# Rotary embedding on one core: four slots of 32 KB for x in place of five, batch 7 loaded and batch 4 stored in halves, the last 1 MB stored as two transfers

## The chip, the cores and the metric

The kernel runs on one core of one Trainium2 chip. The metric is the device time of one execution in microseconds. Before the change the median of three executions is 164.32 us (163.64, 164.32 and 164.39). One further execution was profiled. It took 164.17 us, and its profile spans 162.4 us from the first to the last instruction, so 1.8 us of the time lie outside the span.

## The reference: what is computed

The input `x` has the shape (8, 2048, 8, 64) in float32: 8 batches, 2048 positions, 8 heads, 64 elements a head. `cos` and `sin` have the shape (2048, 32).

```python
x1 = x[..., :32]
x2 = x[..., 32:]
out1 = x1 * cos - x2 * sin
out2 = x1 * sin + x2 * cos
return np.concatenate([out1, out2], axis=-1)
```

`cos` and `sin` are the same for all batches and heads of a position. x is 33.55 MB and so is the output. Each element is read once and written once.

## The kernel before, in words

**Tiling.** A batch is one tile `xt` of 128 partitions by 8192 floats (`ROW`, 32 KB in each partition, 4 MB in all). Partition q holds the 16 positions 16q to 16q+15, each of 512 floats (`HD`), so a partition's row of a batch is one contiguous run of 32 KB in DRAM, both for the load and for the store. The tiles come from `xpool`, which has `NBUF` slots. The rotation is done in place, and the store reads the same tile, so a slot is free for a new batch when the store of the old batch has landed.

**Loads.** `load(b)` issues the loads of batch b on the SP queue. Batch 0 comes as three transfers (1, 1 and 2 MB, rows of 8, 8 and 16 KB) with the table of cosines between them; the other batches come as one transfer of 4 MB with rows of 32 KB. The first `NBUF` batches are loaded ahead of everything (line 77). The load of batch b + `NBUF` is issued after the stores of batch b in program order (line 192); on SP it waits for those stores' landing. SP's instructions stand in a fixed order, so what is behind a waiting load waits too. Two of the early loads also wait for another transfer because eight completion semaphores are handed round: in the kernel before, the load of batch 4 waits for the first 1 MB of batch 0's store.

**Compute.** `rotate` treats a piece of 2048 floats a partition (`UNIT`, four positions); batch 0 begins and batch 7 ends with two pieces of half that. The order on each engine is the program's order (`keep`). There are three kinds of piece. Kind A: POOL makes `t2` in two multiplications (line 122), DVE makes `t1` (line 129) and adds the two into x (line 136). Kind B (the first piece of batches 2, 4 and 5): POOL and DVE make `t2` and `t1`, and TensorE and ScalarE add and copy back. Kind C (the first piece of batches 1 and 3): DVE makes both products, and POOL has none. `t2` has three buffers, so POOL can run at most some pieces ahead of DVE.

**Stores.** `shares(b)` says in which transfers a batch is stored: batch 0 in four of 1 MB, batches 1 to 6 in one of 4 MB each, batch 7 in three of 2, 1 and 1 MB (rows of 16, 8 and 8 KB). Each is issued when its pieces are done. Batches 0 to 6 go out on the ACT queue, batch 7 on the SP queue, behind all the loads. SP's and ACT's queues (q1 and q10 in the profile) feed the same 16 DMA engines.

Of the kernel before, what the change touches and what calls it, by code (L numbers as in the profile page):

```python
# [10 lines left out]
def kernel(  # L11
# [15 lines left out]
    HD = H * D  # L27
    R = S // P
    ROW = R * HD
    UNIT = 4 * HD  # L30
    NBUF = 5
    C = 512
    last = B - 1

# [9 lines left out]
    t1s_pool = ctx.enter_context(tc.tile_pool(name="t1s", bufs=2))  # L44
    xpool = ctx.enter_context(tc.tile_pool(name="xpool", bufs=NBUF))
    t2_pool = ctx.enter_context(tc.tile_pool(name="t2p", bufs=3))
# [11 lines left out]
    def spans(sizes):  # L58
        lo = 0
        for n in sizes:  # L60
            yield lo, n
            lo += n

    def load(b):
        xt = xpool.tile([P, ROW], f32, tag="xt", name=f"xt{b}")
        for lo, n in spans([UNIT, UNIT, 2 * UNIT] if b == 0 else [ROW]):
            keep(nc.sync.dma_start(out=xt[:, lo : lo + n], in_=xv[b, :, lo : lo + n]))
            if b == 0 and lo == 0:
                keep(nc.sync.dma_start(out=cos_sb, in_=cos_src))
        xts[b] = xt  # L70

    def store(b, lo, n):
        queue = nc.sync if b == last else nc.scalar
        keep(queue.dma_start(out=ov[b, :, lo : lo + n], in_=xts[b][:, lo : lo + n]))

    keep(nc.scalar.dma_start(out=sin_sb, in_=sin_src))
    for b in range(NBUF):
        load(b)
# [98 lines left out]
    def shares(b):  # L177
        if b == 0:
            return [UNIT] * 4
        if b == last:  # L180
            return [2 * UNIT, UNIT, UNIT]
        return [ROW]

    for b in range(B):
        done = 0
        outs = list(spans(shares(b)))
        for lo, n in spans(pieces(b)):
            rotate(b, lo, n)
            done = lo + n
            while outs and sum(outs[0]) <= done:  # L190
                store(b, *outs.pop(0))
        if b + NBUF <= last:
            load(b + NBUF)

# [29 lines left out]
```

## Time and profile before

| what | value |
|---|---|
| median of three executions | 164.32 us |
| profiled execution, its own time | 164.17 us |
| span of the profile | 162.4 us |
| DVE busy | 140.1 us, 86% |
| POOL busy | 138.8 us, 85% |
| PE busy, ACT busy | 49.1 us, 12.8 us |
| DMA moved | 67.65 MB, mean 417 GB/s |
| share of 16 engines' span, q1 and q10 | 55.1% and 42.5% |
| last DVE addition ends | 151.89 us |
| last store issued, landed | 151.91 us, 161.49 us |

The trace gives each transfer an issue and a landing (the time at which all 16 DMA engines have reported). In order, in us, with the transfer's size:

```
load 0    0.73, 1.63, 2.10 -> 6.10, 9.25, 14.12   (1, 1, 2 MB)
load 1    2.68 ->  25.86    store 0  12.71 -> 28.88, 18.16 -> 40.97,
load 2    6.11 ->  37.98             22.89 -> 53.17, 27.61 -> 62.90 (1 MB each)
load 3    9.26 ->  50.15    store 1  46.12 ->  78.80
load 4   28.89 ->  62.28    store 2  62.35 ->  99.07
load 5   63.03 ->  86.98    store 3  80.81 -> 118.78
load 6   78.88 -> 106.73    store 4  97.05 -> 132.36
load 7   99.15 -> 126.32    store 5 113.51 -> 142.05
                            store 6 132.47 -> 154.78
                            store 7 142.01 -> 156.60 (2 MB), 146.73 -> 159.04,
                                    151.91 -> 161.49 (1 MB each)
```

A busy share counts an engine's own instructions. The share of a DMA queue counts the time of its packets, summed over the 16 engines; one packet is one partition's row of a transfer, and each engine takes eight of a transfer's 128 rows. Where both queues have work, an engine alternates between them.

### The profile page before, as it was taken

To read this page: it belongs to the slowest core of one execution; us is meant where nothing else is said; L and a number is where in the kernel's file an instruction comes from. 1 tells how busy PE (TensorE), PEld (TensorE's weight loads), DVE (VectorE), ACT (ScalarE), POOL (GpSimd) and SP (SyncE) were. 2 spreads that over 40 slices of the span, in tenths; PEclk is the share of its full clock that TensorE was granted. 3 is DMA by queue.
4 is the path that set the end of the run, shared out by engine and by line. 5 is a ranking of instruction groups with operands and counts; after the bars stand their busy time and mean duration, and the time that the engine had idled before them with its cause. 6 is when DMAs were issued, how large, how long until landed. Compare 5 with 4: busy or idle time off the path is not lost.

```text
span 162.4 us, 462 instructions
## 1 busy us (share of the span) xinstructions
PE 49.1 (30%) x80; PEld 18.5 (11%) x80; DVE 140.1 (86%) x66; ACT 12.8 (8%) x14; POOL 138.8 (85%) x70
## 2 busy tenths in 40 slices
PE   0000000597209750977058805971000000000000
PEld 0000000233003210322022302230000000000000
DVE  0397999999999999999999999999999999999300
ACT  3300000002200220022001120022000000000000
POOL 1499997999999999999995999999999999993000
PEclk9999999999965997589857995699555555555555
DMA  5999799899899899989999999899999999999992
GB/s 182 426 426 517 337 470 452 363 476 460 353 478 468 349 474 476 396 388 509 388 388 501 404 438 460 388 460 438 396 476 420 396 484 412 396 460 428 396 428 113
DMA packets 3602, 67.65 MB, mean 417 GB/s; under 512 B 400, under 2 KB 400, under 8 KB 656
## 3 DMA queue, kind: packets, MB, share of 16 engines
q1 hardware_dynamic: 2016, 38.01, 55.1%
q10 hardware_dynamic: 1584, 29.62, 42.5%
q14 instruction: 2, 0.02, 0.0%
HBM read 34.08 MB, written 33.55 MB: 417 GB/s over the span
## 4 chain that ended last, share of the span: by engine, by line
DVE 75%; POOL 9%; issue 6%; DMA 3%; DVEq 0%
DVE t L129 40%; DVE xt L136 33%; POOL t L122 9%; DMA sin_sb<-in_sin_dram 3%; DVE t L148 3%; DVEq L136 0%
## 5 line engine op out<-in xcount | busy, mean ns | idle before, releaser
L122 POOL TENSOR_TENSOR t<-xt,sin_sb 128x1024 f32<-128x1024 f32 (+1 forms) x32 | 70.7, 2210 | 8.2 <-DMA sin_sb<-in_sin_dram 5.0
L129 DVE TENSOR_TENSOR t<-xt,cos_ps 128x2048 f32<-128x2048 f32 (+1 forms) x34 | 73.4, 2166 | 0.8
L122 POOL TENSOR_TENSOR t<-xt,nsin 128x1024 f32<-128x1024 f32 (+1 forms) x32 | 70.7, 2211 | 0.0
L136 DVE TENSOR_TENSOR xt<-t,t 128x2048 f32<-128x2048 f32 (+1 forms) x29 | 62.2, 2145 | 4.2 <-POOL t L122 1.2
L143 PE MATMUL o<-t,eye 128*128 128x512 f32 x24 | 16.9, 794 | 23.2 <-DVE t L129 19.7
L160 PE MATMUL o<-t,eye 128*128 128x512 f32 x16 | 12.0, 842 | 37.6 <-DVE t L129 35.4
L144 PE MATMUL o<-t,eye 128*128 128x512 f32 x24 | 14.9, 709 | 0.0
L145 ACT COPY xt<-o 128x1024 f32<-128x1024 f32 x6 | 6.1, 1012 | 45.7 <-PE o L144 34.9
L143 PEld LDWEIGHTS o<-t,eye 128*128 128x128 f32 x24 | 5.6, 257 | 32.6 <-issue 26.7
L160 PEld LDWEIGHTS o<-t,eye 128*128 128x128 f32 x16 | 3.7, 257 | 43.1 <-issue 39.2
L165 ACT COPY xt<-o 128x1024 f32<-128x1024 f32 x4 | 4.0, 1012 | 47.7 <-PE o L161 47.7
L144 PEld LDWEIGHTS o<-t,eye 128*128 128x128 f32 x24 | 5.6, 235 | 8.0 <-issue 7.5
L93 DVE COPY cos_ps<-cos_sb 128x512 f32<-128x512 f32 x1 | 0.7, 695 | 6.8 <-DMA cos_sb<-in_cos_dram 6.8
L161 PE MATMUL o<-t,neye 128*128 128x512 f32 x8 | 6.2, 870 | 0.2
L148 DVE TENSOR_TENSOR t<-xt,sin_ps 128x2048 f32<-128x2048 f32 x2 | 4.6, 2280 | 0.0
L161 PE MATMUL o<-t,eye 128*128 128x512 f32 x8 | 4.1, 593 | 0.0
L161 PEld LDWEIGHTS o<-t,neye 128*128 128x128 f32 x8 | 2.1, 294 | 5.2 <-issue 3.6
L161 PEld LDWEIGHTS o<-t,eye 128*128 128x128 f32 x8 | 1.5, 190 | 1.9 <-issue 1.9
L90 ACT ACT_TABLE_LOAD x1 | 1.3, 1283 | 1.2 <-PEq L208 1.2
L90 ACT ACTIVATE nsin<-sin_sb 128x512 f32<-128x512 f32 x1 | 0.6, 629 | 3.9 <-DMA sin_sb<-in_sin_dram 3.9
L91 ACT COPY sin_ps<-sin_sb 128x512 f32<-128x512 f32 x1 | 0.6, 579 | 0.0
L80 POOL MEMSET eye<- 128x128 f32 x1 | 0.2, 206 | 0.3 <-POOLq L208 0.3
(6 smaller groups left out, 1.0 us busy)
## 6 DMA issues: line engine op xcount, KB each, us to landing
xt<-in_x_dram SPq DMA_DIRECT2D x7, 4096.0 KB, 27.9
out_dram<-xt ACTq DMA_DIRECT2D x6, 4096.0 KB, 34.0
out_dram<-xt ACTq DMA_DIRECT2D x4, 1024.0 KB, 26.5
xt<-in_x_dram SPq DMA_DIRECT2D x2, 1024.0 KB, 6.5
xt<-in_x_dram SPq DMA_DIRECT2D x1, 2048.0 KB, 12.0
out_dram<-xt SPq DMA_DIRECT2D x1, 2048.0 KB, 14.6
out_dram<-xt SPq DMA_DIRECT2D x2, 1024.0 KB, 10.9
sin_sb<-in_sin_dram ACTq DMA_DIRECT2D x1, 256.0 KB, 5.5
```

The source lines that it names most:

```text
L90: keep(nc.scalar.mul(nsin, sin_sb, -1.0))
L93: keep(nc.vector.tensor_copy(cos_ps, cos_sb))
L122: nc.gpsimd.tensor_mul(out=t2u[:, :, u, :].rearrange("p (r h) d -> p r h d", h=H), in0=xu[:, :, 1 - u, :].rearrange("p (r h) d -> p r h d" ...
L129: nc.vector.tensor_mul(out=t1.rearrange("p (r k d) -> p r k d", r=nr, d=Dh), in0=xk, in1=rep(cos_ps[:, r0 : r0 + nr, :], 2 * H),)
L136: keep(nc.vector.tensor_add(out=xt, in0=t1, in1=t2))
L143: nc.tensor.matmul(oc, eye, t1[:, cs], start=True, stop=False)
L144: nc.tensor.matmul(oc, eye, t2[:, cs], start=False, stop=True)
L145: keep(nc.scalar.copy(xt[:, 2 * j * C : 2 * (j + 1) * C], o))
L148: nc.vector.tensor_mul(out=t2.rearrange("p (r k d) -> p r k d", r=nr, d=Dh), in0=xk, in1=rep(sin_ps[:, r0 : r0 + nr, :], 2 * H),)
L160: nc.tensor.matmul(oc, eye, t1u[:, gs, u, :], start=True, stop=False)
L161: nc.tensor.matmul(oc, eye if u else neye, t2u[:, gs, 1 - u, :], start=False, stop=True)
L165: nc.scalar.copy(xu[:, :, u, :], o.rearrange("p (g d) -> p g d", d=Dh))
```

## The change

`xpool` has four slots in place of five, which leaves 32 KB of each partition unused. The first four batches are loaded ahead; the load of batch b + 4 waits for the landing of batch b's store. Batch 7 is loaded as two transfers of 2 MB with rows of 16 KB. Batch 4 is stored as two transfers of 2 MB with rows of 16 KB, the first of them after the batch's second piece. The last 1 MB of batch 7 is stored as two transfers of 512 KB with rows of 4 KB, one after each of the two half pieces. The order of the compute instructions on DVE, POOL, TensorE and ScalarE is the same.

```diff
-    NBUF = 5
+    NBUF = 4
@@ load
-        for lo, n in spans([UNIT, UNIT, 2 * UNIT] if b == 0 else [ROW]):
+        for lo, n in spans({0: [UNIT, UNIT, 2 * UNIT], last: [2 * UNIT, 2 * UNIT]}.get(b, [ROW])):
             keep(nc.sync.dma_start(out=xt[:, lo : lo + n], in_=xv[b, :, lo : lo + n]))
@@ shares
         if b == 0:
             return [UNIT] * 4
         if b == last:
-            return [2 * UNIT, UNIT, UNIT]
-        return [ROW]
+            return [2 * UNIT, UNIT, 2 * HD, 2 * HD]
+        return [2 * UNIT, 2 * UNIT] if b in (4,) else [ROW]
```

## The prediction, made before the changed kernel was run

> **What bounds the kernel now.** I read the page's rows on DMA first, because 67.65 MB in 162.4 us is much for one core.
>
> ```profile
> DMA  5999799899899899989999999899999999999992
> ...
> q1 hardware_dynamic: 2016, 38.01, 55.1%
> q10 hardware_dynamic: 1584, 29.62, 42.5%
> ...
> DVE 75%; POOL 9%; issue 6%; DMA 3%; DVEq 0%
> ```
>
> The two queues' packets took 55.1 + 42.5 = 97.6% of 16 engines' span, that is 0.976 x 162.4 = 158.5 us on each engine. The last line, the chain that ended last, says something else: DVE 75%. But that chain is followed back from the last instruction, which is DVE's addition that ends at 151.89 us. The 10.5 us after it are not on the chain; they belong to stores. The table of stretches decides between the two readings (the columns are the stretch, its length, busy time and instructions of PE, PEld, DVE, ACT and POOL, PE's clock, the DMA share, GB/s):
>
> ```profile
> 10.00:25.00 15.00, 0.00 (x0) 0.00 (x0) 13.82 (x8) 0.00 (x0) 14.94 (x8) 1.00 0.99 418
> 63.00:80.00 17.00, 10.15 (x16) 3.64 (x16) 16.62 (x8) 2.02 (x2) 17.00 (x8) 0.80 1.00 430
> 100.00:125.00 25.00, 9.03 (x16) 3.31 (x14) 23.99 (x11) 2.02 (x2) 25.00 (x12) 0.70 0.98 424
> 125.00:142.00 17.00, 0.00 (x0) 0.00 (x0) 16.36 (x8) 0.00 (x0) 17.00 (x8) 0.50 1.00 432
> 142.00:152.00 10.00, 0.00 (x0) 0.00 (x0) 9.49 (x6) 0.00 (x0) 5.65 (x5) 0.50 1.01 434
> 152.00:160.00 8.00, 0.00 (x0) 0.00 (x0) 0.00 (x0) 0.00 (x0) 0.00 (x0) 0.50 0.89 378
> ```
>
> The DMA engines have no idle time from 10 us to 152 us, with loads and stores, with loads alone nearly, and with stores alone. They carry on after the last DVE instruction, and their rate (418 to 434 GB/s) hardly depends on the mix. So the time is the DMA work plus the 1 us before its start and the last landing. Compute matters only where it lets the DMA engines run dry. From the packets, 14 of the engines finish between 159.2 and 159.8 us and the slowest at 161.1 us.
>
> Who waits for slots is in SyncE's waits and in the single issues:
>
> ```profile
> SPq L67 <- DMA out_dram<-xt: 88.1, 4, 33.6
> ...
> 28.89 0.33 SPq L67 DMA_DIRECT2D xt<-in_x_dram  x1
> ...
> 63.03 0.33 SPq L67 DMA_DIRECT2D xt<-in_x_dram  x1
> ...
> 99.15 0.33 SPq L67 DMA_DIRECT2D xt<-in_x_dram  x1
> ...
> 151.91 0.33 SPq L74 DMA_DIRECT2D out_dram<-xt  x1
> ```
>
> The loads of batches 4, 5 and 7 are issued at 28.89, 63.03 and 99.15 us (6 at 78.88), each just after the landing of a store. And two lines show who needs the loads first, and where POOL holds DVE already (POOL's first multiplication for batch 4; DVE's addition for the second piece of batch 5):
>
> ```profile
> 71.79 2.40 POOL L122 TENSOR_TENSOR t<-xt,sin_sb 128x1024 f32<-128x1024 f32 x1
> ...
> 101.70 2.29 DVE L136 TENSOR_TENSOR xt<-t,t 128x2048 f32<-128x2048 f32 x1 [0.33 <-POOL t L122]
> ```
>
> **Part 1: four slots.** Load 4 now waits for all of store 0, and loads 5, 6, 7 for stores 1, 2, 3 in place of 0, 1, 2. They stand in order on SP, so each also waits for those ahead. I work the queue forward by one rule read off the landings: the engines alternate row by row between the queues, and a 4 MB transfer alone takes 4.19 MB / 432 GB/s = 9.7 us (1.21 us a row), beside another of 32 KB rows 19.4 us.
>
> - Load 3 lands at 50.15 us as before. The SP queue is then empty, and the ACT queue has a fifth of store 0's third MB and its fourth MB left, 3 us alone. It ends near 52 and lands near 53.4: load 4 is issued there, 24.5 us later than before.
> - Store 1 (issued at 46.12) runs from 52, alone for three rows, then beside load 4 for five: it ends near 67.8, lands near 69.2. Load 5 is issued there (before: 63.03).
> - Load 5 of before, in the same company, took 86.98 - 63.03 = 23.95 us to land. So load 4 lands near 53.4 + 23.9 = 77.3. Load 6 of before, behind 8 us of another load, took 27.85 us; so load 5 lands near 69.2 + 27.85 = 97.0.
> - Store 2 ends near 67.8 + 19.4 = 87.2, load 6 is issued near 88.6. It has 2:1 company once store 4's 16 KB rows come, and lands near 114.5. Store 3 lands near 108, and load 7's halves land near 124 and 136.
>
> POOL wants load 4 at 71.79 and gets it at 77.3. It runs two multiplications of 2.29 us a piece, so batch 4's second piece is ready at 77.3 + 9.2 = 86.5; DVE's addition there stood at 85.22, so DVE loses 1.3 us. POOL is through with batch 4 at 95.6 and waits for load 5 until 97.1; the second piece of batch 5 is ready at 97.1 + 9.2 = 106.3, where DVE's addition stood at 101.70. DVE is then 4.6 us late in all. Batch 6 is wanted by POOL at 115.4 (there near 114.5) and batch 7 at 133.7 and 142.8 (there at 124 and 136): nothing more. The last addition ends near 151.89 + 4.6 = 156.5 us.
>
> What is this worth? While compute stalls, the DMA engines always have a load and a store, or one whole 4 MB store, in front of them: at 53 store 1, at 69 load 4 and store 2, at 88 load 5 and store 3, at 108 load 6 and store 4, and from 134 on stores 5, 6 and 7, which lie there in stock. So the cost is 0 as long as the last piece comes before the stock is used up. Before, the typical engine had 159.3 - 2.5 (the last 1 MB) = 156.8 us of work without the last transfer, whose issue at 151.91 left 4.9 us less the 1.0 us from issue to first packet (0.73 to 1.73 at the start), so 3.9 us of cover. The delay of 4.6 us takes all of it and 0.7 us more on the typical engine, if nothing else changed. Part 3 gives 1.2 us back. On the slowest engine there are 1.8 us more.
>
> **Part 2: halves of load 7 and store 4.** Two more transfers; each issue takes 0.33 us on a queue that waits anyway (the cover is SyncE's 88.1 us of waits; without it, 0.33 us each). Row prices in the packets: 32 KB 1.213, 16 KB 0.611, 8 KB 0.309 us. Two rows of 16 KB cost 0.009 us more than one of 32 KB, eight rows an engine: 0.07 us for each transfer split, 0.14 us in all, on the path because the DMA engines are. The first half of store 4 leaves some 3 us earlier; as nothing is idle, that moves work and gains nothing.
>
> **Part 3: the last 1 MB in two.** No row of 4 KB is in the trace. Its bounds are half an 8 KB row, 0.1545 us, and two 2 KB rows (the tables'), 0.168 us; a gain is excluded because the bytes stay. Sixteen rows an engine in place of eight of 0.309: +0.0 to +0.22 us. I take 0.158 (the rows of 8 KB are nearest), +0.06 us. Only 512 KB, 1.27 us, now follow the last addition in place of 2.5: the cover grows by 1.2 us.
>
> **Sum.** 0.14 + 0.06 = +0.2 us of DMA work. The last 512 KB is issued near 156.5, its first row is due near 157.5; the typical engine has work until 159.3 + 0.2 - 1.27 = 158.2. The cover is 0.7 us there and 2.5 us on the slowest engine. So the span goes from 162.4 to 162.6, and the profiled execution's 164.17 to 164.4 us, which is the median of before plus 0.05%: no change that can be told. A measurement of this kernel tells about 0.5%, 0.8 us, from nothing.
>
> By the Trainium skill ("SBUF — State Buffer", "The DMA setup-cost knee") every transfer pays a roughly fixed 2 us; with three transfers more that would be 6 us, 170.4 us. The trace has 25 transfers and no idle DMA engine between 10 and 152 us, so here the fixed part lies in latency and not in the engines' time.
>
> **Rivals.**
>
> 1. *The stock runs dry (slower).* Load 5's landing sets POOL, POOL sets DVE, 1:1, and past the cover the end follows 1:1. On the slowest engine it decides from a last addition at 156.5 + 2.5 = 159.0; on typical engines from 157.2, and they become the last ones past 159. For 0.8 us more than the sum it needs about 159.8, that is load 5 landing 3.3 us later than 97.0, or load 6 later than 118. The landings lag by 2 us behind the rows (load 7 of before reports on 16 engines from 124.4 to 126.3), and each slot now hangs on two such lags. A last addition at 160 to 161 would give 165.4 to 166.3. Against it: load times taken from the trace include that lag once.
> 2. *A shorter tail (faster).* If compute set the end, half of the last transfer would gain 1.2 us: 163.0; 161.1 - 159.3 = 1.8 us is also what the slowest engine could lose of its lag, 162.4. For it: compute does end later now. Against: the last store took 9.6 us to land for 2.5 us of work, so there is a queue in front of it.
> 3. *A price for each transfer.* If every transfer held the engines for its latency: the first 1 MB took 5.4 us to land for 2.5 us of moving, 2.9 us more; three times is 8.7 us, 172.9 us. The full shares of DMA in the stretches speak against it.
> 4. *The freed 32 KB does something by itself:* nothing takes it, so 0 us; it falls together with the forecast.
>
> **How the numbers follow.** Forecast, with rival 4: 0.62. Rival 1: 0.24, rival 2: 0.12, rival 3: 0.02. The likeliest case's own range is 163.7 to 165.0 (the three executions of before differ by 0.75 us; part 3's upper end is 0.2 more). The 8-in-10 range reaches down to 163.4, into rival 2, and up to 166.0, into rival 1. Faster by over 0.5% is under 163.5: 0.12; slower is over 165.1: 0.26 (rivals 1 and 3); between them 0.62.
>
> **What would show it.** The DMA share should stay at 0.98 or more in all stretches from 10 to 156 us. Load 4 should be issued near 53.4, 5 near 69, 6 near 89, 7 near 108; POOL should wait about 5.5 us for load 4 and 1.5 us for load 5; DVE's idle time should grow by about 4.6 us and its last addition end near 156.5. The last store should land 4 to 5 us after its issue, in place of 9.6. The prediction is wrong if the share drops below 0.95 in a stretch before 152, or if the last addition ends past 159.

## The result and the profile after

| | before | changed |
|---|---|---|
| median | 164.05 us (20 executions) | 165.05 us (20 executions) |
| profiled execution | 164.17 us, span 162.4 us | 164.47 us, span 162.7 us |
| last DVE addition ends | 151.89 us | 156.48 us |
| last store issued, landed | 151.91, 161.49 us | 156.50, 161.61 us |

The ratio is 1.0061 with a 95% interval of 1.0043 to 1.0079: slower by 0.6%, at the edge of the 0.5% that the prediction took as the least that can be told. Two later comparisons of the same two kernels, on two chips, gave 1.0029 (1.0008 to 1.0051) and 1.0043 (1.0022 to 1.0063). So the change costs some 0.3 to 0.6%, 0.5 to 1.0 us, and the sum of the prediction had 0.2 us. The first profiled execution, at 164.47 us, is one of the faster of its twenty (164.11 to 165.80); its own difference, 0.30 us, agrees with the sum better than the medians do. Of the changed kernel's 20 executions 10 took over 165.0 us, of the 20 before 2.

The DMA rows of the changed kernel's page and, below them, its chain that ended last in order of time (start, length, what):

```profile
q1 hardware_dynamic: 2304, 38.01, 55.1%
q10 hardware_dynamic: 1728, 29.62, 42.5%
...
46.19 23.05 DMA out_dram<-xt
69.38 27.54 DMA xt<-in_x_dram
...
97.05 9.20 POOL t L122 x4
```

The queues' shares are the same to a tenth of a percent, over a span that is 0.3 us longer. The chain now holds what was not on it before: the store of batch 1, then the load of batch 5 into the slot that this store has freed, then POOL's four multiplications for batch 5, and only then DVE.

The stretches of the changed kernel that answer to those shown of before (columns as there), and the waits and issues:

```profile
63.00:80.00 17.00, 9.15 (x16) 3.20 (x16) 16.62 (x8) 2.02 (x2) 11.77 (x6) 0.86 1.00 430
100.00:125.00 25.00, 9.76 (x16) 3.80 (x16) 21.23 (x10) 2.02 (x2) 25.00 (x12) 0.70 1.00 430
125.00:142.00 17.00, 0.00 (x0) 0.00 (x0) 16.35 (x9) 0.00 (x0) 17.00 (x8) 0.50 1.02 438
142.00:152.00 10.00, 0.00 (x0) 0.00 (x0) 9.72 (x5) 0.00 (x0) 10.00 (x7) 0.50 0.96 413
152.00:160.00 8.00, 0.00 (x0) 0.00 (x0) 4.23 (x4) 0.00 (x0) 0.26 (x1) 0.50 0.95 401
```

```profile
SPq L67 <- DMA out_dram<-xt: 93.4, 4, 39.3
...
53.57 0.33 SPq L67 DMA_DIRECT2D xt<-in_x_dram  x1
...
69.38 0.33 SPq L67 DMA_DIRECT2D xt<-in_x_dram  x1
...
77.28 2.32 POOL L122 TENSOR_TENSOR t<-xt,sin_sb 128x1024 f32<-128x1024 f32 x1 [5.24 <-DMA xt<-in_x_dram]
97.05 2.33 POOL L122 TENSOR_TENSOR t<-xt,sin_sb 128x1024 f32<-128x1024 f32 x1 [1.38 <-DMA xt<-in_x_dram]
...
86.51 2.29 DVE L136 TENSOR_TENSOR xt<-t,t 128x2048 f32<-128x2048 f32 x1 [1.31 <-POOL t L122]
106.28 2.29 DVE L136 TENSOR_TENSOR xt<-t,t 128x2048 f32<-128x2048 f32 x1 [3.22 <-POOL t L122]
...
156.50 0.33 SPq L74 DMA_DIRECT2D out_dram<-xt  x1
```

POOL waits 5.24 us for batch 4 and 1.38 us for batch 5, DVE then 1.31 and 3.22 us for POOL, and the last store is issued at 156.50 us in place of 151.91. POOL's busy time from 63 to 80 us falls from 17.00 to 11.77 us, DVE's from 100 to 125 us from 23.99 to 21.23 us, while the DMA share is 1.00 in both stretches. From 142 to 152 us it reads 0.96: a packet counts whole in the stretch in which it begins, and by the packet records no engine is idle there. Compute is late by 4.6 us, and the DMA engines do not notice it in this execution. This profile accounts for 0.3 us. What is left to find is why the medians differ by more.

### The profile page after: what moved, and what is told of

Its sections match the earlier page's. It is cut to its first block, busy times and chain, and to the rows that moved or that the text cites. A ratio compares the mean times of both kernels' runs of the same rounds, so it can differ in the third digit from the quotient of the medians.

```text
span 162.7 us, 472 instructions
## 1 busy us (share of the span) xinstructions
PE 49.0 (30%) x80; PEld 18.3 (11%) x80; DVE 140.1 (86%) x66; ACT 12.8 (8%) x14; POOL 138.9 (85%) x70
## 3 DMA queue, kind: packets, MB, share of 16 engines
q1 hardware_dynamic: 2304, 38.01, 55.1%
q10 hardware_dynamic: 1728, 29.62, 42.5%
## 4 chain that ended last, share of the span: by engine, by line
DVE 48%; DMA 35%; POOL 11%; issue 1%; DVEq 0%; SPq 0%; POOLq 0%; ACTq 0%
DVE xt L136 24%; DVE t L129 23%; DMA xt<-in_x_dram 17%; DMA out_dram<-xt 14%; POOL t L122 11%; DMA sin_sb<-in_sin_dram 3%; DVE t L148 1%; DVEq L136 0%; SPq L67 0%; POOLq L122 0%; ACTq L74 0%
```

## The experiments

The theories, as they were named at the time: **A**, the late last addition uses up the cover at the end; **B**, the splits cost more than their packets show; **C**, four slots lengthen the slowest DMA engine's lag, whenever compute ends; **D**, a finer form of A, in which the last addition stands just at the edge of the cover and lags of landings push it over; **E**, lateness and splits together. All ratios are to the kernel before, beside which each ran.

| run | slots | splits | last addition ends (its profile) | ratio, 95% interval |
|---|---|---|---|---|
| e1 | 4 | no | 158.4 us | 1.0065, 1.0039 to 1.0091 |
| e2, e11 | 5 | yes | 152.1, 152.5 us | 1.0015, 0.9998 to 1.0033; 1.0021, 0.9997 to 1.0045 |
| e3, e10 | 4 | yes | 153.7, 154.4 us | 1.0033, 1.0007 to 1.0060; 1.0083, 1.0057 to 1.0110 |
| e4 | 5 | no | 156.5 us | 0.9985, 0.9967 to 1.0003 |
| e6 | 5 | yes | 156.8 us | 1.0031, 1.0000 to 1.0062 |
| changed, e7, e9 | 4 | yes | 156.5, 157.8, 157.8 us | 1.0061; 1.0029; 1.0043 |
| e12 | 5 | yes | 158.9 us | 1.0047, 1.0030 to 1.0065 |
| e5 | 4 | yes | 159.6 us | 1.0129, 1.0092 to 1.0166 |

Runs e1 to e4 shared one chip, e5 to e8 a second, e9 to e12 a third. e8 is the changed kernel profiled once more: one execution, 164.59 us, last addition at 157.5 us.

### Four slots alone, and the splits alone

```diff
 e1, from before:    -    NBUF = 5          +    NBUF = 4
 e2, from changed:   -    NBUF = 4          +    NBUF = 5
```

> Four slots alone: load 7, store 4 and the last 1 MB stay whole. Theory A (the cover at the end is used up: the last addition comes some 4.6 us later, and the DMA engines have little or nothing left to do when the last transfer is issued): load 7 whole lands near 136 where POOL wants it near 134, so the last addition comes near 157.5 to 158.5, and 1 MB instead of 512 KB follows it; the ratio to the kernel before is 1.010 to 1.020, worse than the changed kernel's 1.006. Theory B (the three more transfers and the smaller rows cost more than their packets show): 0.998 to 1.002. Theory C (four slots make the slowest DMA engine's lag longer, through the waits for landings, whenever compute ends): about 1.005.

> The three splits with five slots. Theory A: the last addition stays near 151.9 us, the work of the splits is 0.2 to 0.3 us, ratio 1.000 to 1.003. Theory B: the splits carry the loss, 1.004 to 1.008. Theory C: 1.000 to 1.003 as well; e3 tells A from C.

Four slots alone gave 1.0065, the splits alone 1.0015. So the splits cost about what the sum said (0.15% is 0.25 us, the interval runs from 0 to 0.5 us, and the sum had 0.2 us), and B falls as the main cause. In this pair the slots carry the rest. In e1 the load of batch 7, whole, landed at 136.7 us and the last addition came at 158.39, as A expected. The last microseconds (one stretch each, columns as before) show what follows:

```profile
157.00:158.00 1.00, 0.00 (x0) 0.00 (x0) 0.90 (x2) 0.00 (x0) 0.00 (x0) 0.50 0.83 352
158.00:159.00 1.00, 0.00 (x0) 0.00 (x0) 0.40 (x1) 0.00 (x0) 0.00 (x0) 0.50 0.14 57
159.00:160.00 1.00, 0.00 (x0) 0.00 (x0) 0.00 (x0) 0.00 (x0) 0.00 (x0) 0.50 0.90 377
160.00:161.00 1.00, 0.00 (x0) 0.00 (x0) 0.00 (x0) 0.00 (x0) 0.00 (x0) 0.50 1.01 410
```

The DMA share drops to 0.14 for a microsecond: nothing is in front of the engines until the last 1 MB, issued at 158.42, arrives. That is the dry spell of rival 1, in the kernel without the splits. A's size was too large all the same (1.010 to 1.020 expected). The same stretch of the changed kernel's first profile:

```profile
158.00:159.00 1.00, 0.00 (x0) 0.00 (x0) 0.00 (x0) 0.00 (x0) 0.00 (x0) 0.50 1.01 414
```

So in this execution the halves of load 7 and of the last 1 MB do keep the engines from running dry.

### Compute early with four slots, compute late with five

```diff
 e3, from changed, in rotate:
         kind = kinds.get((b, lo), "A")
+        if b == 6 and lo in (UNIT, 2 * UNIT):
+            n = n // 2
 e4, from before, after the multiplication of line 129:
+        if b == 5 and lo in (UNIT, 2 * UNIT):
+            keep(nc.vector.tensor_mul(...))      # the same once more
```

> The changed kernel with two pieces of batch 6 rotated in their first half only (the other half of these two pieces goes out as it came in), so that DVE and POOL have 4.7 and 4.6 us less to do and the last addition comes near 151.9 us again; loads, stores, slots and their waits are those of the changed kernel. Theory A: the loss goes but for the splits' work, ratio 1.000 to 1.003. Theories B and C: the loss stays, 1.004 to 1.008.

> The kernel before with two multiplications on DVE made twice (two pieces of batch 5), so that DVE has 4.4 to 4.7 us more and the last addition comes near 156.4 us; slots and transfers are those of before. Theory A: the cover of 3.9 us is used up and the last 1 MB (2.5 us) follows late; typical engines run dry for 0.5 to 2 us, the span grows by 0.5 to 2 us, ratio 1.004 to 1.012. Theories B and C: 0.998 to 1.002, as DMA is untouched.

e4 is the clearest run of the study: with the last addition at 156.52 us and a whole 1 MB behind it, the ratio is 0.9985, no loss. So a last addition at 156.5 us does not cost anything by itself, and A falls for that lateness. The last microseconds show why:

```profile
157.00:158.00 1.00, 0.00 (x0) 0.00 (x0) 0.00 (x0) 0.00 (x0) 0.00 (x0) 0.50 0.76 320
158.00:159.00 1.00, 0.00 (x0) 0.00 (x0) 0.00 (x0) 0.00 (x0) 0.00 (x0) 0.50 1.09 451
159.00:160.00 1.00, 0.00 (x0) 0.00 (x0) 0.00 (x0) 0.00 (x0) 0.00 (x0) 0.50 0.84 344
160.00:161.00 1.00, 0.00 (x0) 0.00 (x0) 0.00 (x0) 0.00 (x0) 0.00 (x0) 0.50 0.12 49
```

Most engines do run dry, for about half a microsecond near 157.5 (share 0.76). They then end near 160.0 us by the packet records, and the slowest engine, which never ran dry, at 161.04. A share of 0.12 in the last microsecond is as much work as two of sixteen engines do: that of the slowest, and the rests of three that end near 160.5. The slowest engine sets the end, so up to a point a dry spell on the others is free.

e3, four slots with compute early because half of two pieces is left out, gave 1.0033 (1.0007 to 1.0060). It lies between what A and C expected and decides nothing.

### The edge: more lateness, and the same lateness with five slots

```diff
 e5, from changed, after line 129:              +        if b == 6 and lo == UNIT:                 # multiply once more
 e6, from the splits with five slots, likewise: +        if b == 5 and lo in (UNIT, 2 * UNIT):    # multiply once more
```

> The changed kernel with one multiplication on DVE made twice (a piece of batch 6): the last addition 2.2 to 2.3 us later, near 158.8 in a run like the profiled one. Theory D (with four slots the last addition stands at the edge: lags of load landings move it 1:1, and in a typical run it already sets the end): 1.5 to 2.3 us over the changed kernel, ratio to the kernel before 1.015 to 1.020. If the slowest DMA engine sets the end as in the profiled run (Theory C: four slots lengthen that engine's lag whenever compute ends), 0 to 0.5 us more, ratio 1.006 to 1.010.

> The three splits with five slots, and two multiplications on DVE made twice (batch 5), so that the last addition comes near 156.4 us as in the changed kernel, but without hanging on the landing of loads. Theory D: the end stays with the slowest DMA engine, ratio 1.000 to 1.003, as the splits alone gave (1.0015). A rival E (lateness and the splits together, the small last transfers above all, cost the time, whatever the slots): 1.004 to 1.008, as the changed kernel.

> The changed kernel once more, for its time beside the others and for a second profile. Theory D: a run whose span is over 163.0 us shows a last addition later than 156.5 us by 0.5 us or more, with loads 4 or 5 landing as much later, and idle DMA engines of 0.3 to 1.5 us before the last transfer. Theory C: such a run shows the last addition at 156.5 and one engine ending past 161.5 us without idle time.

> The changed kernel a third time, for a third profile; what each theory expects is as for the second: Theory D ties a longer span to a later last addition and later landings of loads 4 and 5, Theory C to the slowest engine alone.

e5 gave 1.0129: one multiplication of 2.3 us more cost 1.1 us over the changed kernel beside it by the medians (165.58 against 164.48 us) and 1.6 us by the ratios. Past the changed kernel's lateness the end does follow compute. How nearly 1:1 can't be read from this run: part of the 2.3 us may still be covered, and longer rows of store 7 (last section) add 0.8 us an engine. e6, with five slots and the changed kernel's lateness, gave 1.0031, which can't be told from the changed kernel's 1.0029 beside it. Its interval reaches over what D and what E expected; for the splits, lateness and five slots together it leaves at most 0.6%.

The second profile of the changed kernel (span 162.5) had POOL's waits at 6.87 and 0.98 us and the last store issued at 157.78, the third (162.8) at 157.50, 1.0 to 1.3 us later than in the first. So the lag of load landings does move compute from execution to execution, as D says. But neither showed more than two idle engines, for 0.1 us, before the last transfer, the execution with the latest addition had the shortest span, and neither span was over the 163.0 us for which the two theories differed. D is not borne out by these two, and C is not tested by them.

### The last comparison on one chip

```diff
 e9:   the changed kernel        e10:  e3 once more        e11:  e2 once more
 e12, from e6:
-        if b == 5 and lo in (UNIT, 2 * UNIT):
+        if b == 5 and lo > 0:
```

> The changed kernel, on one chip with the next three, because its ratio was 1.0061 (1.0043 to 1.0079) in one comparison and 1.0029 (1.0008 to 1.0051) in another. Whatever the cause, 1.003 to 1.006.

> Four slots with two pieces of batch 6 rotated in their first half only (the rest of them goes out as it came in), last addition near 152 to 154 us. Theory D (lateness at the edge of the cover): below the changed kernel beside it by 0.1% to 0.4%, and within 0.15% of the five-slot splits. Theory C (the slots themselves): the same as the changed kernel within 0.1%, and 0.2% or more above the five-slot splits.

> The three splits with five slots, last addition near 152 us: ratio 1.000 to 1.003 in both theories; it is the level against which the two others of this chip are held.

> The three splits with five slots and three multiplications on DVE made twice (batch 5), so that the last addition comes near 158.8 us, where the changed kernel with one such multiplication (ratio 1.0129) had it. Theory D: lateness decides and the slots matter through it alone, ratio 1.009 to 1.016. Theory C: with five slots the same lateness costs little, 1.002 to 1.006.

e10 contradicts D: compute early gave 1.0083 (1.0057 to 1.0110), not below the changed kernel's 1.0043 but above it, and clear of the five-slot splits' 1.0021 (0.9997 to 1.0045). D expected it below. e12 contradicts D as well: with five slots a last addition at 158.92 us cost 1.0047, where D had 1.009 to 1.016. C expected e12 right and missed e10's size. Its form, that four slots cost something by themselves, stays possible, but it is not shown. e3 and e10 are the same kernel and gave 1.0033 and 1.0083, so two comparisons can differ by as much as the whole effect. On the second chip, with splits and late compute in both, four slots (e7, 1.0029) and five (e6, 1.0031) gave the same.

One profile shows how an execution can lose time, e10's (165.68 us), from the issue of its load 5 to its last microseconds:

```profile
71.89 0.33 SPq L67 DMA_DIRECT2D xt<-in_x_dram  x1
...
159.00:160.00 1.00, 0.00 (x0) 0.00 (x0) 0.00 (x0) 0.00 (x0) 0.00 (x0) 0.50 0.76 311
160.00:161.00 1.00, 0.00 (x0) 0.00 (x0) 0.00 (x0) 0.00 (x0) 0.00 (x0) 0.50 0.09 37
161.00:162.00 1.00, 0.00 (x0) 0.00 (x0) 0.00 (x0) 0.00 (x0) 0.00 (x0) 0.50 0.07 29
162.00:163.00 1.00, 0.00 (x0) 0.00 (x0) 0.00 (x0) 0.00 (x0) 0.00 (x0) 0.50 0.02 8
```

For the last two microseconds one engine of sixteen works (0.07 is about 1/16). By the packet records fifteen engines end between 159.5 and 160.4 us and one at 162.4. That engine's lag is old: store 1 reported from the first engine at 66.2 us and from the last at 71.8, and load 5, which waits for all sixteen, was issued at 71.89 in place of 69.38. Part of it is older than the change's effect: load 3, up to which four and five slots have the same loads, landed on fifteen engines by 50.30 us and on the last at 51.65. So 1.35 us of such a lag need no missing slot; at the end the last engine is 2.07 us behind the fifteenth. The jump to 5.2 us at store 1 is for the most part order and not lost work. When load 4's rows came in between, this engine, late by 1.75 us, had moved four of store 1's eight rows and the others six, so two more load rows (1.36 and 2.44 us, both lengthened) stood before its report.

In e9's own profile the last store was issued at 157.79 us and seven engines were idle for 0.1 to 0.5 us before its first rows, so in some executions the changed kernel does touch the edge; its slowest engine, at 161.45, had not been idle.

The slowest engine's end in the profiles in which nothing ran dry for all: with five slots 161.1, 161.3, 161.7, 161.0 and 161.0 us (before, e2, e11, e6, e4), mean 161.2; with four 161.3, 161.0, 161.4, 161.5, 161.7 and 162.4 (the changed kernel four times, e3, e10), mean 161.5. The difference of 0.3 us has the sign of C, but it is smaller than the spread. Before and e4 have no splits; against the three five-slot profiles with them (mean 161.3) it is 0.2 us, and without e10 (mean of the others 161.4) almost nothing is left.

## Why the prediction came out as it did

The profiled execution, 164.47 us, is where the forecast had it (164.4). The median, 165.05 us, lies 0.65 us above: inside the 8-in-10 range, but just over the likeliest case's own range (163.7 to 165.0). That the execution which was profiled is one of the faster is luck.

**What bounds the kernel** was right. DMA carries 55.1 + 42.5% before and after, and a compute that ends 4.6 us later cost nothing where it was tried alone (e4).

**Part 1, the queue worked forward,** was right to 0.3 us as far as load 5, and to about 1 us after. Load 4 was issued at 53.57 us (53.4 forecast) and landed at 77.15 (77.3); load 5 at 69.38 (69.2), landed 96.92 (97.0); load 6 at 89.31 (88.6), landed 114.83 (114.5); load 7 at 109.10 (108), its halves landed at 124.55 and 136.08 (124 and 136). POOL waited 5.24 and 1.38 us (5.5 and 1.5), and the last addition ended at 156.48 (156.5). The rule of rows in turn was enough for this. That the last addition came out to the tenth is partly luck: in the three later profiles of the changed kernel it ended at 157.5 to 157.8 us, and POOL waited 5.9 to 6.9 us for batch 4. Two signs were missed by little: the last store landed 5.1 us after its issue (4 to 5 forecast), and the stretch from 142 to 152 us reads 0.96 where 0.98 was forecast, without an idle engine in the packet records.

**Part 1, what it is worth,** is the step that was mis-sized: "So the cost is 0 as long as the last piece comes before the stock is used up." In the profiled execution it was near 0 (0.30 us in all, 0.2 of it the sum's for the splits). In the medians the changed kernel costs more than the splits alone, by 0.1 to 0.5% or 0.1 to 0.75 us (1.0029 to 1.0061 against 1.0015 and 1.0021). On the one chip that had both, 1.0043 against 1.0021, the intervals overlap. Making compute early did not give the loss back (e3, e10), so the stock alone doesn't explain it; five slots with splits and late compute did not give it back either (1.0031 and 1.0047 in e6 and e12). Which part of it four slots cause, if any, stays open.

The forecast was drawn from one execution's lags, and those differ between executions. The extra time of lengthened rows is 1.1 us an engine in the profiles of before and after, and 1.3 to 1.8 us in the three later ones of the changed kernel. But with five slots it is 1.0, 1.8 and 1.9 us as well (e2, e11, e6), and the changed kernel's shortest span, 162.5 us, is the one with 1.8. So this time does not by itself set the end: the slowest engine does. None of the changed kernel's four profiles is of an execution over 165.0 us (164.30 to 164.66), so what the longer ones lose has not been seen.

**Parts 2 and 3** were right: 0.14 + 0.06 = 0.2 us against 0.25 us (1.0015) and 0.34 us (1.0021) measured, both within their intervals. The 4 KB row took 0.159 us, 0.158 was taken.

**Rival 1** had its mechanism right and its edge nearly so. It decides from a last addition at 159.0 on the slowest engine, the prediction said; e12 with 158.9 lost some 0.3% beyond its splits, e5 with 159.6 lost 1.3% in all. That is more than the 0.6 us past the edge; 0.8 us an engine of it are the longer rows of the last section. The changed kernel, at 156.5 to 157.8, is short of it. **Rival 2** fell: halving the last transfer made nothing faster. **Rival 3** fell with e2 and e11: three transfers more cost 0.25 to 0.34 us together.

By the Trainium skill ("SBUF — State Buffer", "The DMA setup-cost knee") a transfer pays a roughly fixed 2 us, an estimated 6 us for three if they add up. In e2 and e11 they don't: 0.25 and 0.34 us. The section calls the fixed part mostly completion latency, and the DMA shares near 1.00 fit that.

## What to carry to other kernels

Where the DMA engines are busy throughout, work the transfers forward row by row to see when buffers come free, and compare the last compute instruction with the slowest engine's stock of work and not with the average's: here lateness was free up to there (e4), and past it 2.3 us more cost 1.1 to 1.6 us (e5). A buffer that only prefetches was worth between nothing and some 0.65% (e1) in this kernel. The wait for a slot is a wait for the slowest of sixteen engines (66.2 to 71.8 us in e10). Judge an effect of half a percent by medians over several comparisons: one profile of a kernel lay 0.6 us off its median here, and two ratios of one kernel differed by 0.3 and by 0.5%.

## What the runs showed that was not expected

**The first rows of store 7 are longer where they begin soon after its issue.** In e5 and e12 store 7 was issued when most engines were at their last row of store 6, and its first 16 KB rows began 1.1 to 1.7 us after the issue. They took 1.3 to 1.6 us in place of 0.611, on nearly every engine. In e1 four of the five first rows that began within 1.7 us took 1.5 to 1.7 us. In all profiles the first rows that began 1.75 us or more after the issue took 0.61 us. An idle time before a row is not what does it: rows that follow one directly took their usual time (32 KB 1.21 to 1.22 us at 140 us in e5 and e12, 8 KB 0.31 to 0.32 us at 158 us in e1). The cause was not tried. The stretch from 150 to 151 us, before first, then e12:

```profile
150.00:151.00 1.00, 0.00 (x0) 0.00 (x0) 0.90 (x2) 0.00 (x0) 0.00 (x0) 0.50 1.06 459
```

```profile
150.00:151.00 1.00, 0.00 (x0) 0.00 (x0) 1.00 (x1) 0.00 (x0) 1.00 (x2) 0.50 1.39 262
```

Over one microsecond either column swings with where rows begin (e10 reads 0.57 at 246 GB/s without a longer row), but the two together give the time that a byte took: it is 2.3 times as long in e12. The longer rows cost 0.78 us an engine in e12 and 0.84 us in e5, which a busy share alone would hide.

**Bursts of lengthened rows.** Rows of 32 KB take 1.213 us but for bursts in which they take 1.4 to 2.6 us on many engines at once. They come mostly at 66 to 68 us with four slots and at 76 to 78 us with five, where store 1 ends beside a load, and they are worth from 0.1 to 1.0 us an engine, differing from execution to execution of the same kernel (0.1 and 1.0 us in the first and second profile of the changed one). The time does not follow them: the second profile has the shorter span, 162.5 against 162.7 us. What causes them was not tried.
